# A two-stage recurrent layer on one core: the first stage put in a written order of twelve slots per pair of tiles, its arithmetic taken off GpSimd, and one norm moved to the second stage

## The chip, the cores and the metric

The kernel runs on one core of a Trainium2 chip. A core has five engines that run side by side, each through its own list of instructions in order: TensorE (PE in the profile; PEld is its loading of weights), VectorE (DVE), ScalarE (ACT), GpSimd (POOL) and SyncE (SP), which here only starts transfers. They wait for one another by semaphores. The metric is the device time of one execution in microseconds (us). The kernel before was run three times: 2977.22, 2985.96 and 2986.02 us, so its median is 2985.96 us.

## The reference

One layer over a prompt of 4096 tokens and eight short sequences of 16 tokens, 1024 channels wide:

```
h    = rmsnorm(x, norm_w);  proj = h @ w_in
# group A, gated delta rule, 8 heads of 64
q,k,v = silu(causal_conv(proj[qkv], width 4)); q, k = l2norm(q)/8, l2norm(k)
g    = -exp(A_log) * softplus(a + dt_bias);  beta = sigmoid(b)
#   per chunk: decay = exp(G_i - G_j) for j <= i, G = cumsum(g)
#   lower = strict part of (beta k) k^T * decay; solve (I + lower) [u, w] = rhs
#   v_new = u - w S;  o = (q exp(G)) S + (q k^T * decay) v_new
#   S = S exp(G_last) + (k exp(G_last - G))^T v_new
o_a  = rmsnorm(o, gdn_norm_w) * silu(z_a)        # per head
# group B, HGRN2, 4 heads of 128: forget gate f by channel, same kind of chunked recurrence
o_b  = rmsnorm(o, hgrn_norm_w) * silu(z_b)
y    = rmsnorm(x + concat(o_a, o_b) @ w_out, final_norm_w)
```

The outputs are y for prompt and sequences, the last rows before the convolution, and the final states of both groups.

## The kernel before

The prompt is cut into 32 tiles of 128 tokens; the eight short sequences make one more tile. A group is a pair of prompt tiles, or that one tile: the lone tile comes first, then 16 pairs. Group A runs over all groups in a first stage, group B, the output projection and the last norm in a second one, since both keep the weights of their projections in SBUF.

All projections are done as three fp16 products: weights and x are each split into a high and a low part, and `mm3` (L462–464) adds high·high, high·low and low·high. In the first stage that makes 12 blocks of 128 channels, each 24 matmuls of 128x256 for a pair. What happens to a pair:

- `xload` and `xtrans` (L346–383) load x, norm it (`xss` is the row scale, a power taken by GpSimd at L361, applied at L362) and transpose it into two fp16 parts `xt`. `gate` and `gate2` work out beta and the decays: a polynomial of small operations on VectorE (L405–430), and G along the free axis, sent through DRAM as `gdr`.
- `proj` (L466–515), per block: ScalarE scales the sum `acc` into `u` (L493) and makes two of the four taps of the convolution (L504 from `acc`, L507 from `u`); GpSimd adds these two (L508) and keeps the last three columns in `halo` (L492, L494); VectorE adds the two other taps (L510); ScalarE's tanh (L512) and one VectorE operation (L514) finish silu into `kq` or `vv`.
- `gdn_pre` (L517–582): G is broadcast from DRAM into `E`; GpSimd subtracts (L539) and masks (L540), ScalarE exponentiates; k by token is squared and summed head by head on ScalarE (L554, eight operations with an accumulator per tile); the scores `pk` on TensorE times `E` give `W` and `A` on VectorE (L573, L574); the 32x32 blocks of `W` go to DRAM (`wdr`, L577). `gdn_pre2` makes q and v by token (L594, L600), and GpSimd multiplies `kq` by exp(G) (L602, L603).
- `gdn_inv` (L605–672) inverts the 32x32 triangular blocks of both tiles at once, one system on two partitions. `N` is read back from `wdr` with a transfer that spreads it over the partitions (L623); VectorE scales it (L632) and runs 31 steps of two operations each, L636 (`tm` from `X` and `N`) and L638 (`X` minus `tm`), each needing the one before. `X` then goes through DRAM (`xdr`) into `tx`; VectorE transposes it (L656) and TensorE couples the blocks (`pv`, `px`).
- `gdn_rec` (L674–771) is the recurrence for one tile: `pks` and `po` from the state `S`, then `r` (L713), `py`, `w`, `pcr`, `r` (L723), `pz`, `w`, `pss`, and `S` (GpSimd times its decay at L690, VectorE plus `pss` at L737), each needing the last, back and forth between TensorE, VectorE and ScalarE. The norm of o by head follows: eight squares on ScalarE (L765), a power on GpSimd (L767), a multiplication on VectorE (L769), and `oa` to DRAM (L771).
- `wspill` (L131 on) prepares the weights of the second stage meanwhile, by pieces of 128 columns: GpSimd multiplies by the norm weights (L146) and makes the low part (L185), ScalarE squares and casts; the parts go to DRAM. The first stage's own weights are prepared ahead of its loop by `wprep` (the norm weights at L120, the low part at L129).

The loop over the groups calls these for different groups (transposes for g+2, projection for g+1, preparation for g, recurrence for g−1), but that order is only a suggestion: a scheduler, which simulates the engines with a cost model, decides the order on every engine in both stages. Buffers come from pools that rotate. The second stage (`hg_proj`, `hg_levels`, `hg_tok`, `hg_tile`) is ordered by the same scheduler.

Of the kernel before, what the change touches and what calls it, by code (L numbers as in the profile page):

```python
# [22 lines left out]
XS = 1024.0  # L23


class Kern:
# [10 lines left out]
    # ---------------------------------------------------------------- consts  # L37
    def consts(self, ctx):
# [15 lines left out]
        # small vectors as rows, transposed on the tensor engine  # L54
        i = self.i
        rows = cp.tile([66, P], F32, tag="rows", name="rows")
        nc.sync.dma_start(rows[0:48], i["conv_w"][0].rearrange("t (b p) -> (t b) p", p=P))
        nc.sync.dma_start(rows[48:56], i["norm_w"][0].rearrange("(b p) -> b p", p=P))
        nc.sync.dma_start(rows[56:64], i["hgrn_lb_logits"].rearrange("t (b p) -> (t b) p", p=P))
        nc.sync.dma_start(rows[64:65, 0:64], i["gdn_norm_w"])  # L60
        nc.sync.dma_start(rows[64:65, 64:128], i["gdn_norm_w"])
        nc.sync.dma_start(rows[65:66], i["hgrn_norm_w"])
        self.cols = ct("cols", [P, 66])
        with tc.tile_pool(name="cps", bufs=1, space=PSUM) as pp:
            t = pp.tile([P, 66], F32, tag="t", name="cps_t")
            nc.tensor.transpose(t, rows, self.ident[0:66, 0:66])
            nc.scalar.copy(self.cols, t)
        self.nw = self.cols[:, 48:56]
        self.wosc = self.cols[:, 64:66]
        # conv taps times one half: [p, tap, block]  # L70
# [3 lines left out]
        # -2 exp(A_log), dt_bias on all partitions  # L74
# [6 lines left out]

    def masks(self):
# [3 lines left out]
        # mi[t, i] = t <= i  # L86
# [3 lines left out]
        # sequence of a token of the sample tile: sm[t, s], b16[t, i], ms[t, i] = b16 and t <= i  # L90
# [12 lines left out]
    # --------------------------------------------------------------- weights  # L103
    def wscale(self, tot, us, s2, oscale, small, nm):
        """s2, a power of two: the fp16 parts of weights with that sum of squares; us = oscale / s2"""
# [6 lines left out]
        nc.vector.tensor_scalar(us, us, oscale, None, ALU.mult)  # L112

    def wprep(self, c0, c1, hi, lo, us, stg, eng):
        """hi + lo = (rows of w_in scaled by norm_w) * s in fp16 parts, us = 1 / (s * XS), s a power of two."""
# [4 lines left out]
        eng.tensor_tensor(st, st, self.nw[:, :, None].to_broadcast([P, NDC, w]), ALU.mult)  # L120
# [6 lines left out]
        self.wscale(tot, us, s2, 1.0 / XS, small, c0)  # L127
# [3 lines left out]
    def wspill(self):  # L131
        """the same for the weights of phase B, to DRAM in fp16 parts, by steps of 128 columns"""
# [7 lines left out]
        fac = {}  # L140

        def stage(nm, src, c):
            st = self.ex.tile([P, NDC, P], F32, tag="st", name=f"st{nm}{c}")
            with self.tc.issue_after(self.mark.ins):
                nc.sync.dma_start(st, src[:, :, c:c + P])
            nc.gpsimd.tensor_tensor(st, st, fac[nm][:, :, None].to_broadcast([P, NDC, P]), ALU.mult)  # L146
            return st

        for nm, src, c0 in names:
            fac[nm] = wrow if src is wout else self.nw  # L150
            self.wd[nm] = self.wdp.tile([P, 2, NDC, 512], F16, tag=f"wd{nm}", name=f"wd{nm}")
            ssq = w.tile([P, 4], F32, tag=f"ssq{nm}", name=f"ssq{nm}")
            if nm == "o0":
                # rows of w_out: norm weight of the head and what the gate left out
# [4 lines left out]
            for c in range(4):  # L159
                st = stage(nm, src, c0 + c * P)  # L160
                nc.scalar.activation(st, st, AF.Square, accum_out=ssq[:, c:c + 1])
                yield
# [1030 lines left out]
```

## Time and profile before

| | |
|---|---|
| times of three runs | 2977.22, 2985.96, 2986.02 us |
| the profiled execution's span | 2983.5 us |
| mean granted TensorE clock | 0.943 |
| busy over the span | PE 87%, DVE 59%, ACT 41%, POOL 33% |
| stages, read from where the groups' projections end | to 155.2 us: weights, the lone tile's and the first pair's projection; to 1436.3: the other 15 projections; to 1600: the last pair's rest and the second stage's start; to 2983.5: the second stage |

The profiled execution's own time is not stated apart from its span; the span runs from its first to its last instruction and lies within the range of the runs. Times in the trace count from the span's start. The profile has the busy time and the idle time of each engine, what ended each idle time, and groups of instructions by source line; a duration of a matmul includes its way through a pipeline, so the pitch between neighbours is what it costs. A clock of 1 is TensorE at full speed; 0.5 would be half.

### The profile page before, as it was taken

Reading aid. Unit: us, or ns where it says so; the run is one execution under the profiler, and the core shown is the slowest. Engines: PE = TensorE matmul, PEld = TensorE weight load, DVE = VectorE, ACT = ScalarE, POOL = GpSimd, SP = SyncE. Lnnn points to the kernel's source line nnn. Section 1 sums busy time; section 2 is a strip of 40 time slices with the busy share of each in tenths; the row PEclk is TensorE's granted clock in tenths of the full one; section 3 lists DMA queues with packets and bytes.
Section 4 is the critical chain, followed back from the end, with each engine's and each line's share of the span. In section 5 each row is a group of like instructions: output and inputs, shape, how many; then the busy total and the mean of one; then the engine's idle time right before and its main releaser. Section 6 shows DMA issues by size and latency. Waiting matters only on the chain.

```text
span 2983.5 us, 67579 instructions
## 1 busy us (share of the span) xinstructions
PE 2598.1 (87%) x27628; PEld 1847.4 (62%) x27628; DVE 1752.2 (59%) x4215; ACT 1219.2 (41%) x3930; POOL 991.0 (33%) x1300
## 2 busy tenths in 40 slices
PE   4768678877877887778899999999999999999997
PEld 4656566665666666666674666666656666665664
DVE  7786778777778788876644434444433344433343
ACT  6656565555555665555332222222222222222222
POOL 5755565465565665655320001110001111000110
PEclk9888999888898989888999999999999999999999
DMA  6334232233343333333233231111110111111010
GB/s 180 100 100 122 68 107 74 73 101 106 98 121 77 96 103 99 97 94 115 77 92 112 73 98 40 43 51 44 51 47 24 46 44 50 44 51 34 32 37 33
DMA packets 298701, 227.78 MB, mean 76 GB/s; under 512 B 186409, under 2 KB 263614, under 8 KB 293782
## 3 DMA queue, kind: packets, MB, share of 16 engines
q1 hardware_dynamic: 298390, 223.45, 25.6%
q8 instruction: 217, 3.56, 0.5%
q14 instruction: 94, 0.77, 0.1%
HBM read 151.78 MB, written 71.62 MB: 75 GB/s over the span
## 4 chain that ended last, share of the span: by engine, by line
PE 49%; DVE 28%; DMA 13%; ACT 2%; issue 2%; POOL 2%; SPq 2%; DVEq 0%; POOLq 0%; ACTq 0%
DMA N<-wdr 7%; DVE X L638 6%; DVE c L510 5%; DVE tm L636 5%; PE py L1016 4%; PE py L1014 4%; PE py L1015 4%; PE hac L462 4%; PE hac L464 4%; PE hac L463 4%; PE sc L954 2%; PE tpzb L1014 2%; PE tpza L1014 2%; PE tpzb L1015 2%; PE tpzb L1016 2%
## 5 line engine op out<-in xcount | busy, mean ns | idle before, releaser
L462 PE MATMUL acc<-xt,w 128*128 128x256 f16 (+1 forms) x1632 | 468.9, 289 | 38.5 <-ACT c L504 36.8
L464 PE MATMUL acc<-xt,w 128*128 128x256 f16 (+1 forms) x1632 | 468.0, 288 | 2.7 <-DVE w L129 2.7
L463 PE MATMUL acc<-xt,w 128*128 128x256 f16 (+1 forms) x1632 | 468.9, 289 | 0.0
L510 DVE SCALAR_TENSOR_TENSOR c<-u,cw,c 128x256 f32<-128x256 f32 (+1 forms) x408 | 237.0, 584 | 31.0 <-POOL c L508 29.8
L1145 DVE SCALAR_TENSOR_TENSOR xr<-py,ysc,xr 128x512 f32<-128x512 f32 x66 | 49.5, 750 | 302.3 <-PE py L1016 302.3
L638 DVE TENSOR_TENSOR X<-X,tm 128x126 f32<-128x126 f32 (+26 forms) x527 | 220.5, 418 | 7.3
L512 ACT ACTIVATE c<-c 128x256 f32<-128x256 f32 (+1 forms) x204 | 83.4, 409 | 322.3 <-DVE c L510 197.6
L463 PEld LDWEIGHTS <-w 128*128 128x128 f16 x1632 | 171.9, 105 | 67.8 <-issue 41.3
L1014 PE MATMUL py<-wo,oh 128*128 128x512 f16 x528 | 201.0, 381 | 4.7 <-ACT oh L1137 3.5
L1016 PE MATMUL py<-wo,ol 128*128 128x512 f16 x528 | 201.1, 381 | 0.2
L1015 PE MATMUL py<-wo,oh 128*128 128x512 f16 x528 | 201.0, 381 | 0.0
L462 PEld LDWEIGHTS <-w 128*128 128x128 f16 x1632 | 172.2, 106 | 37.6 <-issue 9.9
L464 PEld LDWEIGHTS <-w 128*128 128x128 f16 x1632 | 172.0, 105 | 33.5 <-issue 3.3
L636 DVE TENSOR_TENSOR tm<-X,N 128x126 f32<-128x126 f32 (+26 forms) x527 | 187.9, 357 | 7.1
L1048 POOL TENSOR_TENSOR zs<-zs,pw_m 128x1 f32<-128x1 f32 x33 | 20.9, 632 | 469.6 <-DVE zs L1047 469.6
L508 POOL TENSOR_TENSOR c<-c,c 128x256 f32<-128x256 f32 (+1 forms) x204 | 155.9, 766 | 50.9 <-ACT c L507 41.8
L462 PE MATMUL hac<-bxt,whq 128*128 128x256 f16 (+1 forms) x544 | 147.4, 273 | 9.0 <-DVE q L924 9.0
L463 PE MATMUL hac<-bxt,whq 128*128 128x256 f16 (+1 forms) x544 | 147.2, 273 | 0.0
L464 PE MATMUL hac<-bxt,whq 128*128 128x256 f16 (+1 forms) x544 | 147.0, 273 | 0.0
L462 PE MATMUL hac<-bxt,whf 128*128 128x256 f16 (+1 forms) x544 | 145.4, 270 | 0.0
L464 PE MATMUL hac<-bxt,whf 128*128 128x256 f16 (+1 forms) x544 | 145.4, 270 | 0.0
L463 PE MATMUL hac<-bxt,whf 128*128 128x256 f16 (+1 forms) x544 | 145.3, 270 | 0.0
(399 smaller groups left out, 6692.3 us busy)
## 6 DMA issues: line engine op xcount, KB each, us to landing
E<-gdr SPq DMA_DIRECT2D x33, 512.0 KB
out_dram<-xr SPq DMA_DIRECT2D x33, 512.0 KB
x<-in_x_prompt_dram SPq DMA_DIRECT2D x32, 512.0 KB
xd<-xt SPq DMA_DIRECT2D x16, 1024.0 KB
bxt<-xd SPq DMA_DIRECT2D x16, 1024.0 KB
xr<-in_x_prompt_dram SPq DMA_DIRECT2D x32, 512.0 KB
tx<-xdr SPq DMA_DIRECT2D x66, 128.0 KB
oa<-on SPq DMA_DIRECT2D x33, 256.0 KB
```

Source lines behind the costliest of these rows:

```text
L462: nc.tensor.matmul(out, wh[k], xh[k], start=(k == 0), stop=False)
L463: nc.tensor.matmul(out, wh[k], xl[k], start=False, stop=False)
L464: nc.tensor.matmul(out, wl[k], xh[k], start=False, stop=(k == n - 1))
L508: nc.gpsimd.tensor_tensor(c, c, c0, ALU.add)
L510: nc.vector.scalar_tensor_tensor(cv, taps[j], self.cw[:, j, b:b + 1], cv, ALU.mult, ALU.add)
L512: nc.scalar.activation(th, c, AF.Tanh)
L636: nc.vector.tensor_tensor(tv, X[:, 0:R, m:m + 1].to_broadcast([2 * SY, R, c]), N[:, m:m + 1, m + 1:32].to_broadcast([2 * SY, R, c]), ALU.mult)
L638: nc.vector.tensor_tensor(X[:, 0:R, m + 1:32], X[:, 0:R, m + 1:32], tv, ALU.subtract)
L954: nc.tensor.matmul(ps[b:b + 32, k, h], KS[:, k, h, b:b + 32], rhs(k, h, slice(b, b + 32)), start=True, stop=True, tile_position=(0, b))
L1014: nc.tensor.matmul(acc, xh[:, dc], wh[dc], start=(dc == 0), stop=False)
L1015: nc.tensor.matmul(acc, xh[:, dc], wl[dc], start=False, stop=False)
L1016: nc.tensor.matmul(acc, xl[:, dc], wh[dc], start=False, stop=(dc == NDC - 1))
```

## The change

The first stage's loop runs under `manual_schedule`: on every engine the instructions keep the order in which the code writes them. The loop over g has 12 slots. In each slot come, in this order: one step of the recurrence of group g−1, the convolution's pending operations, a second step of the recurrence, one block of the projection of g+1 (24 matmuls), one step each of the preparation of g (which goes on into the next round's first slots), of the gates of g+1 and of the transposes of g+2, and in four of the twelve slots a unit of the spill of weights. The rest after the last round, and the second stage, are still left to the scheduler.

What GpSimd computed moves: the third tap becomes a VectorE operation (three L594 per block, one ScalarE tap less), and two blocks share the `u`, tanh and silu operations; E − G becomes a bias of ScalarE's exponential, head by head (16 operations for 2 a pair); the products by exp(G) go to VectorE (L703), the decay of `S` is fused with its addition (L846, eight operations of 64x64 for two of 64x256 and one on GpSimd); the spill's low parts go to VectorE (L197). The norm weights are multiplied into x (L373) and no longer into the weights. GpSimd keeps masks, powers and small copies. The squares by head become one ScalarE square and one VectorE sum over heads (L608). The norm of o leaves the first stage: it stores o and 8 columns of `nrm` (520 columns for 512), and the second stage's `hg_tok` squares, sums, takes the power and multiplies.

```diff
+            with tc.manual_schedule():
+                for g in range(-1, ng):
+                    rec = self.gdn_rec(g - 1, st.pop(g - 1), oa) if g >= 1 else iter(())
...
+                    for s in range(NSLOT):
+                        next(rec, None)
+                        self.conv_jobs()
+                        next(rec, None)
+                        if g + 1 < ng:
+                            self.proj(g + 1, st[g + 1], s)
+                        for it in (*pre, gat, xs):
+                            next(it, None)
+                        if g >= 0 and s in after:
+                            next(spill, None)
...
-                nc.gpsimd.tensor_tensor(lo, st, hi, ALU.subtract)
...
+                nc.scalar.activation(hi, st, AF.Copy, scale=s2[nm])
+                nc.vector.scalar_tensor_tensor(lo, st, s2[nm], hi, ALU.mult, ALU.subtract)
...
-        nc.vector.tensor_scalar(x, x, ss[:, 1:2], None, ALU.mult)
...
+        nc.vector.scalar_tensor_tensor(x, x, ss[:, 1:2], self.nwb, ALU.mult, ALU.mult)
...
+                nc.scalar.activation(E[:, k, h], E[:, k, h], AF.Exp, bias=nG[:, k, h:h + 1])
...
-            nc.gpsimd.tensor_tensor(c, c, c0, ALU.add)
-            for j in (1, 2):
-                nc.vector.scalar_tensor_tensor(cv, taps[j], self.cw[:, j, b:b + 1], cv, ALU.mult, ALU.add)
...
+        for e in range(2):
+            for j in (1, 2, 3):
+                nc.vector.scalar_tensor_tensor(cv[e], taps[e][j], self.cw[:, j, b + e:b + e + 1], cv[e],
+                                               ALU.mult, ALU.add)
...
+    def sums(self, out, x, sq):
+
+        self.nc.scalar.activation(sq, x, AF.Square)
+        yield
+        self.nc.vector.tensor_reduce(out, sq, AX.X, ALU.add)
...
-        nc.gpsimd.tensor_tensor(E, E, d["G"][:, k, :, None].to_broadcast([P, 8, P]), ALU.subtract)
...
-        nc.gpsimd.tensor_tensor(kq[:, k, 4:8], kq[:, k, 4:8], eg, ALU.mult)
-        nc.gpsimd.tensor_tensor(kq[:, k, 0:4], kq[:, k, 0:4], eg, ALU.mult)
...
+            nc.vector.tensor_tensor(qk, qk, d["eg"][k][:, None].to_broadcast([P, 2, 4, P]), ALU.mult)
...
+            if m in (6, 13, 21):
+                yield
...
-                nc.vector.tensor_tensor(S[q, :, q], S[q, :, q], pss[q], ALU.add)
+                for p in range(4):
+                    nc.vector.scalar_tensor_tensor(S[q, p, q], S[q, p, q], el[q, p, DEC_B - 1:], pss[q, p],
+                                                   ALU.mult, ALU.add)
...
-            nc.scalar.activation(junk, po[:, h * 64:(h + 1) * 64], AF.Square, accum_out=n[:, 0, h:h + 1])
...
+        nc.scalar.copy(on[:, 0:512], po)
+        nc.scalar.copy(on[:, 512:520], nrm[:, k, 0:8])
+        nc.sync.dma_start(oa[self.groups[g][k]], on)
...
+            sq = self.ex.tile([P, 8, 64], F32, tag="st", name=f"sq{nm}", bufs=1)
+            o3 = on[:, 0:512].rearrange("p (h d) -> p h d", h=8)
+            nc.scalar.activation(sq, o3, AF.Square)
+            n8 = sm.tile([P, 2, 8], F32, tag="n8", name=f"n8{nm}")
+            nc.vector.tensor_reduce(n8[:, 0], sq, AX.X, ALU.add)
+            nc.vector.scalar_tensor_tensor(n8[:, 0], n8[:, 0], 1.0 / 64, on[:, 512:520], ALU.mult, ALU.add)
+            nc.gpsimd.tensor_tensor(n8[:, 1], n8[:, 0], self.pw_m[:, 0:8], ALU.pow)
+            nc.vector.tensor_tensor(o3, o3, n8[:, 1, :, None].to_broadcast([P, 8, 64]), ALU.mult)
```

How the order changes is seen at three places. Over the whole program VectorE has 4669 instructions for 4217, ScalarE 2044 for 2874, GpSimd 644 for 1302; TensorE and SyncE have as many as before.

VectorE in the middle of the elimination of a pair, before (L636 and L638 are a step's two operations; L376, L514 and L510 belong to other pairs' transposes and convolution):

```order
L376 TENSOR_TENSOR xt_9722<-xtr_0_10265,xt_9722 128x4x128
L636 TENSOR_TENSOR tm_10018<-X_10017,N_10015 128x100
L514 SCALAR_TENSOR_TENSOR kq_10343<-c_0_10528,c_0_10523 128x2x128
L638 TENSOR_TENSOR X_10017<-X_10017,tm_10018 128x4x25
L376 TENSOR_TENSOR xt_9722<-xtr_1_10272,xt_9722 128x4x128
L636 TENSOR_TENSOR tm_10018<-X_10017,N_10015 128x96
```

The same place after the change (L710 and L712 are the two operations):

```order
L710 TENSOR_TENSOR tm_10045<-X_10044,N_10042 128x31
L712 TENSOR_TENSOR X_10044<-X_10044,tm_10045 128x31
L710 TENSOR_TENSOR tm_10045<-X_10044,N_10042 128x30
L712 TENSOR_TENSOR X_10044<-X_10044,tm_10045 128x30
L710 TENSOR_TENSOR tm_10045<-X_10044,N_10042 128x58
L712 TENSOR_TENSOR X_10044<-X_10044,tm_10045 128x2x29
```

Operations of other parts stood between the steps; now the steps of one slot stand one behind the other, in four runs of 14, 14, 16 and 18 operations.

VectorE between the last `W` of a pair, whose store `N` is read back from, and the scaling of `N`; before:

```order
L573 TENSOR_TENSOR WA_1_9988<-pk_1_1_9996,E_9908 128x2x2x128
L574 TENSOR_TENSOR WA_1_9988<-pk_1_1_9996,E_9908 128x2x2x128
L510 SCALAR_TENSOR_TENSOR c_6_10447<-u_6_10446,cw,c_6_10447 128x256
L360 TENSOR_SCALAR xss_10200<-xss_10200 128x1
L510 SCALAR_TENSOR_TENSOR c_6_10447<-u_6_10446,cw,c_6_10447 128x256
L362 TENSOR_SCALAR x_10198<-x_10198,xss_10200 128x1024
L600 TENSOR_TENSOR kv_0_9932<-vt_0_10220,sqk_9906 128x512
L514 SCALAR_TENSOR_TENSOR kq_10343<-c_6_10452,c_6_10447 128x2x128
L596 TENSOR_SCALAR nrm_9905<-nrm_9905 128x8
L600 TENSOR_TENSOR kv_1_9982<-vt_1_10243,sqk_9906 128x512
L632 TENSOR_TENSOR N_10015<-N_10015,cs_10016 128x1024
```

After the change, the last 11 of the 20 rows that stand between the last `W` (L632 there) and the scaling of `N` (L706), and that row:

```order
L700 TENSOR_TENSOR kv_0_9694<-vt_0_10062,sqk_9687 128x512
L703 TENSOR_TENSOR kq_8654<-kq_8654,eg_0_9372 128x1024
L487 TENSOR_TENSOR dec_10141<-nG_10072 128x16
L370 TENSOR_SCALAR xss_10144<-xss_10144 128x1
L602 SCALAR_TENSOR_TENSOR kq_9658<-kq_9658,c_6_10001 128x2x256
L594 SCALAR_TENSOR_TENSOR c_0_10175<-u_0_10174,cw,c_0_10175 128x2x128 x3
L846 SCALAR_TENSOR_TENSOR S<-S,el_0_8462,pss_0_10148 64x64 x8
L608 TENSOR_REDUCE nrm_9686<-sq_1_10134 128x8
L699 TENSOR_SCALAR nrm_9686<-nrm_9686 128x8
L700 TENSOR_TENSOR kv_1_9914<-vt_1_10136,sqk_9687 128x512
L703 TENSOR_TENSOR kq_8654<-kq_8654,eg_1_9378 128x1024
L706 TENSOR_TENSOR N_10042<-N_10042,cs_10043 128x1024
```

The nine rows not shown hold a silu (L602), six taps (L594), an `r` (L819), a norm of x (L373), a low part of the spill (L197), a sum over heads (L608) and two small ones: eight operations stood in this place before, and 33 do now (a row with x3 or x8 is that many).

TensorE at the start of a slot after the change (`pk`, `px` end the slot before; `pks` and `po` begin a tile's recurrence; the rows after them are the projection's next block):

```order
L753 MATMUL px_9802<-tx_0_9452,V_9739 32x32 x16
L753 MATMUL px_9802<-tx_1_9455,V_9739 32x32 x16
L779 MATMUL pks_9861<-S,kq_7650 128x128 x4
L781 MATMUL po_9860<-S,kq_7650 128x128 x4
L525 LDWEIGHTS w_181
L525 MATMUL acc_6_9884<-xt_8746,w_181 128x256
L526 LDWEIGHTS w_181
L526 MATMUL acc_6_9884<-xt_8746,w_181 128x256
```

The block's 24 matmuls stand between `pks`, whose result VectorE turns into `r`, and `py`, which needs `r`. So it is with each of the recurrence's four trips between TensorE and another engine.

More of the change, by code (lines that the diff above doesn't have):

```diff
@@ L1 @@
+from collections import deque
 from contextlib import ExitStack
@@ L325, in phase_a @@
+            akq.close()
+            self.b_begin(xd)
+            for it in (*pre, self.gdn_rec(ng - 1, st.pop(ng - 1), oa)):
+                for _ in it:
+                    pass
             for par in range(2):
```

648 lines of the change are left out of this document (352 added, 296 removed).

## The prediction

> **What bounds the kernel now.** I first read the table by stretches: the stretch's length, then busy time (and count) of PE, PEld, DVE, ACT and POOL, the granted clock, the share and rate of the DMA engines.
>
> ```profile
> 0.00:155.20 155.20, 94.62 (x841) 78.69 (x842) 120.39 (x308) 95.45 (x252) 98.62 (x126) 0.90 0.49 138
> 155.20:1436.30 1281.10, 996.71 (x11283) 815.84 (x11283) 1002.05 (x2449) 742.63 (x2684) 726.95 (x959) 0.89 0.36 99
> 1436.30:1600.00 163.70, 142.43 (x1803) 102.35 (x1799) 80.01 (x224) 49.34 (x194) 35.69 (x44) 0.95 0.33 96
> 1600.00:2983.50 1383.50, 1364.32 (x13711) 850.50 (x13709) 549.80 (x1237) 331.81 (x802) 129.74 (x172) 1.00 0.14 47
> ```
>
> The second stage is TensorE's: 1364 of 1383.5 us. The first is nobody's, with PE and DVE level at 78% and two engines behind. Its second row covers 15 pairs, 85.4 us each (1281.1/15): PE 66.4, DVE 66.8 busy and 18.6 idle, ACT 49.5, POOL 48.5. The same stretch, for the projection's sums alone, PE then ACT:
>
> ```profile
> 155.20:1436.30 1281.10, 570.37 (x4288) 155.66 (x360) 0.89 0.36 99
> ```
>
> That is 38.0 us of PE per pair, so 28.4 us for the rest. What DVE waited for there (us in all, times, longest):
>
> ```profile
> DVE N L632 <- DMA N<-wdr: 143.7, 14, 13.3
> DVE tT L656 <- DMA tx<-xdr: 41.1, 22, 4.2
> DVE c L510 <- POOL c L508: 25.5, 19, 3.4
> ```
>
> Per pair 9.6, 2.7 and 1.7 us: 14.0 of the 18.6. The chain of waits over one pair shows the first (start, length):
>
> ```profile
> 1280.26 0.61 DVE WA L573
> ...
> 1285.11 13.06 DMA N<-wdr
> ```
>
> From the start of the last W to the landing of N pass 17.9 us (1285.11 + 13.06 − 1280.26), and DVE runs dry before that. So DVE's time, busy plus these waits, sets the pair.
>
> **GpSimd inside DVE's busy time.** The same stretch by groups (busy, mean ns | idle), and then minimum, median and maximum of single instructions over the run:
>
> ```profile
> L510 DVE SCALAR_TENSOR_TENSOR c<-u,cw,c 128x256 f32<-128x256 f32 x362 | 213.3, 592 | 26.6 <-POOL c L508 25.5
> L638 DVE TENSOR_TENSOR X<-X,tm 128x126 f32<-128x126 f32 (+23 forms) x469 | 200.1, 427 | 6.1
> L636 DVE TENSOR_TENSOR tm<-X,N 128x126 f32<-128x126 f32 (+23 forms) x468 | 167.7, 358 | 5.9
> L514 DVE SCALAR_TENSOR_TENSOR kq<-c,c 128x256 f32<-128x256 f32 x120 | 68.6, 572 | 7.4 <-ACT c L512 7.2
> ```
>
> ```profile
> L510 DVE SCALAR_TENSOR_TENSOR c<-u,cw,c x408: 336/478/2354, 48.9 to 1432.6; 128x256 f32<-128x256 f32 x128, 128x128 f32<-128x128 f32 x8
> L638 DVE TENSOR_TENSOR X<-X,tm x527: 158/273/2255, 108.5 to 1486.3; 128x126 f32<-128x126 f32 x16, 128x78 f32<-128x78 f32 x11, 128x120 f32<-128x120 f32 x11, 128x96 f32<-128x96 f32 x11
> L636 DVE TENSOR_TENSOR tm<-X,N x527: 158/265/2196, 108.0 to 1486.1; 128x126 f32<-128x126 f32 x16, 128x78 f32<-128x78 f32 x11, 128x120 f32<-128x120 f32 x11, 128x96 f32<-128x96 f32 x11
> L514 DVE SCALAR_TENSOR_TENSOR kq<-c,c x136: 292/418/2309, 54.0 to 1416.6; 128x256 f32<-128x256 f32 x128, 128x128 f32<-128x128 f32 x8
> ```
>
> The means lie far above the medians: 362×0.114 + 469×0.154 + 468×0.093 + 120×0.154 = 41 + 72 + 44 + 18 = 175 us, 11.7 per pair. The timeline says why: a DVE row of 1.98 us, then the GpSimd row beside it.
>
> ```profile
> 798.98 0.48 DVE L510 SCALAR_TENSOR_TENSOR c<-u,cw,c 128x256 f32<-128x256 f32 x1
> 799.38 0.24 DVE L636 TENSOR_TENSOR tm<-X,N 128x78 f32<-128x78 f32 x1
> ...
> 803.39 1.98 DVE L638 TENSOR_TENSOR X<-X,tm 128x115 f32<-128x115 f32 x1
> ...
> 842.16 0.99 DVE L510 SCALAR_TENSOR_TENSOR c<-u,cw,c 128x256 f32<-128x256 f32 x2
> ```
>
> ```profile
> 803.35 1.90 POOL L539 TENSOR_TENSOR E<-E,Gc 128x1024 f32<-128x1024 f32 x1 [0.42 <-ACT eg L538]
> ```
>
> GpSimd starts 0.04 us ahead, and DVE's L638, some 0.27 us of work, ends 0.12 us after it. With the groups not shown I put the stall at 16 us per pair, an estimate (11.7 is its lower bound).
>
> By the Trainium skill (SBUF — State Buffer, the list under its diagram) a VectorE instruction with two SBUF inputs and a GpSimd instruction that reads SBUF lock each other out for a whole instruction; the row above agrees (1.98 us), and by that the masks would go on stalling.
>
> **The change, DVE per pair.** Three more rows give prices, the fourth what GpSimd still does beside small ones:
>
> ```profile
> L573 DVE TENSOR_TENSOR WA<-pk,E 128x512 f32<-128x512 f32 x59 | 40.3, 682 | 0.5 <-PE pk L571 0.2
> L737 DVE TENSOR_TENSOR S<-S,pss 64x256 f32<-64x256 f32 x56 | 23.3, 416 | 1.4 <-PE pss L733 0.5
> L632 DVE TENSOR_TENSOR N<-N,cs 128x1024 f32<-128x1024 f32 x15 | 19.0, 1269 | 153.4 <-DMA N<-wdr 143.7 <-DMA cs<-cdr 9.8
> ```
>
> ```profile
> L540 POOL TENSOR_SCALAR_AFFINE_SELECT E<-E 128x1024 f32<-128x1024 f32 x30 | 34.7, 1156 | 0.0
> ```
>
> - Taps: the tap at 798.98 lets the next operation, which doesn't need it, start after 0.40 us, 0.08 before its own end; the two at 842.16, the second needing the first, take 0.99, a pitch of 0.51. Before 24×0.40 = 9.6; now three in a chain for each of 12 blocks, 12×(0.51+0.51+0.40) = 17.0: **+7.4**.
> - Elimination: the same 62 operations, now each behind the one it needs, so up to 0.11 us more each, 6.8. Some stood so before (the order shows it at 128x96): **+4** (0 to 6.8).
> - Four sums over heads at L573's 0.68: **+2.7**. Two products by exp(G) at L632's 1.27: **+2.5**.
> - S: sixteen of 64x64, no row of that size; the smallest operations take 0.16 (the minimum of L636), 16×0.17 = 2.7 for 4×0.42 = 1.7: **+1.0** (up to +5 at L737's 0.42 each).
> - Spill: 28 low parts and 16 products with the weights of the output, 44×1.27/15: **+3.7**. The norm weights make x's product a two-tensor operation: **+0.5** (up to 2.5, L632's whole price twice). Norm of o: **−1.7** (two of L573's size, two small).
> - Stalls: of the arithmetic 16 us go; the masks stay, 2×1.16 us of GpSimd for E, of which I let 1.5 stall: **−14.5** (−10 to −16).
>
> Sum +5.6, so 66.8 becomes 72.4 busy. On ScalarE a tap goes, squares lose their accumulators, sixteen exponentials come: it stays under its 49.5 and doesn't bound. PE's work is the same 66.4.
>
> **DVE's waits.** Of the 18.6, taps no longer wait for GpSimd (−1.7). `tx` is used three slots after its load is issued, 20 us at 82/12 a slot, against a wait of at most 4.2: −2.7. Between the last W and N stand 33 operations for 8: nine taps 4.3, two silu of 512 1.4, `r` 0.7, x, the spill's part and two exp(G) products 5.1, two sums and two L700 2.7, S 1.4, small ones 0.8: 16.4 against 17.3 us from the end of W. But SyncE's list is fixed too: N's load stands there behind the stores of W, two stores and a load of the spill and the store of the factors `cs`, whose transpose PE makes behind the slot's block of the projection, 38.0/12 = 3.2 us; if PE isn't ahead, N is that much later (and cs with it), and the elimination, and everything DVE has queued behind L706, waits. I leave 1.5 of the 9.6 (0 to 4). The other 4.6 of the 18.6 stay. New are waits that a fixed order makes: DVE may stand before an operation whose producer is late though others are ready. The nearest row is L514's idle above, 7.2 us in 15 pairs; a chain through one `pk` buffer and two through GpSimd's powers come to about 3.5 a pair at some 0.5 to 1 each. Bounds: 0, and what the rivals say. So P = 72.4 + 1.5 + 4.6 + 3.5 = 82.0 us, −3.4 × 15 = **−51**.
>
> **Outside the loop.** Scaling the first weights goes (DVE, then GpSimd, to 155.2 us):
>
> ```profile
> L120 DVE TENSOR_TENSOR wst<-wst,cols 128x2048 f32<-128x2048 f32 (+1 forms) x4 | 7.1, 1787 | 2.1 <-DMA wst<-in_w_in_dram 2.1
> ```
>
> ```profile
> L120 POOL TENSOR_TENSOR wst<-wst,cols 128x2048 f32<-128x2048 f32 x3 | 12.5, 4160 | 2.9 <-DMA wst<-in_w_in_dram 2.9
> ```
>
> At most 20 us, at least none: I take −10. The 163.7 us between the stages keep their scheduler and their work: 0. In the second stage 33 tiles get two DVE operations of 0.68, an ACT square and a GpSimd power, under a TensorE busy 98.6%, with DVE 60% idle: +3 (0 to 20). Total −51 − 10 + 3 = −58 from the profiled 2983.5: 2925.5 us. That execution's span is 2.5 under the median of the runs, so I say **2928**.
>
> **Rivals.**
>
> *Nearly no waits.* If the order is good enough that the new waits and most of the 4.6 go, P is about 75.5: −149 − 7, 2828. For it: 24 matmuls stand between every two steps of the recurrence. Against: each engine's list is strict now.
>
> *The chained order is free.* Then the +4 and 24×0.11 = 2.6 of the taps vanish: P 75.4, −150 − 7, 2827. The 0.99 for two taps against 0.40 for one speaks against it. The Trainium skill says so (VectorE: DVE Perf Modes, The DRAIN you can't avoid: the next operation waits until the pipeline is empty, and a semaphore between costs nothing more); the rows differ, since at 799.38 the next operation started 0.08 us before the recorded end.
>
> *The trips of the recurrence stall both lists.* What PE waited for before:
>
> ```profile
> PE py L718 <- DVE r L713: 38.5, 10, 12.4
> PE pz L726 <- DVE r L723: 20.4, 9, 5.7
> PE pks L685 <- DVE S L737: 19.9, 8, 6.4
> ```
>
> On average 2.9 us (78.8/27). A scheduler put these waits anywhere; now eight trips per pair each stand before a block, and behind a late `r` wait py, the block after it, the sums of the convolution and then DVE. PE has little slack to catch up when it then runs slower (0.89 granted already). If four of the eight trips cost DVE 2.9 us, the new waits are 11.6 for 3.5, P 90.1: +70 − 7, 3047. It decides from new waits of about 7.5 us. For it: the 62 chained operations, 62×0.30 = 19 us, lie in four slots, so with a third of the other 53 DVE has 37 us there against 27 of a pair's 82, while PE's blocks are even. Against: the block between.
>
> *The stalls are not GpSimd's arithmetic.* Without the 14.5, P is 96.5: +166 − 7, 3143. The pair of rows at 803 speaks against.
>
> *The second stage waits for o.* ScalarE's square of `on` must wait for its load, and behind it stand the casts that TensorE needs; at 2.9 us a tile, 33×2.9 = 96: 3022. Against: ACT there is busy 24%, and a scheduler still orders it.
>
> *It cancels:* new waits of 6.5 to 8 us, within 0.3% of 2986.
>
> **Chances.** Forecast 0.50, with its own range 2873 to 2971 (new waits 0 to 6.5); nearly no waits 0.14; free chains 0.05; cancels 0.09; trips 0.14; second stage 0.05; stalls elsewhere 0.03. A measurement tells about 0.3% from no change: faster 0.50 + 0.14 + 0.05 = 0.69, same 0.09, slower 0.22. The range, 2815 to 3040, holds both cheap cases and the second stage's, and leaves out half of the trips, the stalls elsewhere and the tails of the cheap cases, under 2 in 10.
>
> **What would show it.** The step from one pair's projection to the next near 82 us; DVE busy near 72 in it; median and mean of the taps and the elimination together, with long ones only beside the masks; the wait of L706 for N under 4 us; no wait for GpSimd's sum. PE waiting for `r` in most pairs, or a lower clock than 0.89, would be the trips; a TensorE share well under 98.6% after 1600 us the second stage. The prediction is wrong if DVE's idle time a pair is over 13 us, or its busy time over 76.

## The result: 2.3% slower

| | median us | runs |
|---|---|---|
| before | 2984.73 | 2977.22 to 2986.02 |
| after the change | 3050.49 | 3048.78 to 3060.57 |

The median of before now counts the profiled execution, 2983.5, as a fourth time. The ratio is 1.023, with a 95% interval of 1.021 to 1.025. The prediction was 2928 us, with a range up to 3040: wrong in sign, and just outside its range.

The stretch of the profile after that holds the 15 pairs, and the second stage; the columns are as in the prediction's first view. The cuts of the 15 pairs, here and in the table ahead of the change, were counted from another zero than the traces' rows and stand 11 us late: from the span's start the first and the last pair's projections end at 150.7 and 1495.7 us (144.0 and 1425.0 before, not 155.2 and 1436.3). The stretches have the right length, and VectorE's busy time in them is the same within 1 us.

```profile
161.80:1507.00 1345.20, 1018.35 (x11370) 856.10 (x11368) 1084.50 (x2788) 566.77 (x1226) 195.34 (x349) 0.87 0.34 95
```

```profile
1665.00:3049.10 1384.10, 1364.12 (x13704) 849.86 (x13702) 586.73 (x1326) 345.63 (x830) 182.56 (x202) 1.00 0.14 47
```

A pair takes 1345.2/15 = 89.7 us (85.4 before): VectorE is busy for 72.3 and idle for 17.4, TensorE busy for 67.9. The second stage stays at its 1384 us with TensorE busy 98.6%, so the norm that moved there costs nothing that shows. Of the 65.6 us by which the profiled span grew (3049.1 − 2983.5), 64 lie in these 15 pairs, 6.7 ahead of them and −5 behind.

What VectorE waits for in that stretch (us in all, times, longest):

```profile
DVE c L594 <- ACT c L591: 61.4, 53, 3.2
DVE xss L370 <- ACT xt L367: 58.6, 14, 7.7
DVE WA L632 <- PE pk L627: 31.9, 30, 2.7
...
DVE tT L737 <- DMA tx<-xdr: 3.6, 7, 1.0
DVE N L706 <- DMA cs<-cdr: 3.5, 1, 3.5
```

The three waits of before are gone: `N` had 143.7 us and now has one wait of 3.5, `tx` had 41.1 and has 3.6, GpSimd's tap isn't there. In their place stand three that were small before: the taps behind ScalarE's first tap (no such wait before), x's norm behind ScalarE's square of x (5.0 us before), and `W` behind the scores (0.2). Together they are 151.9 us, 10.1 a pair.

### The profile page after: what moved, and what is told of

It is laid out like the page before. It is cut to its first block, busy times and chain, and to the rows that moved or that the text cites. A ratio compares the mean times of both kernels' runs of the same rounds, so it can differ in the third digit from the quotient of the medians.

```text
span 3049.1 us, 65219 instructions
## 1 busy us (share of the span) xinstructions
PE 2618.9 (86%) x27628; PEld 1885.2 (62%) x27628; DVE 1867.5 (61%) x4667; ACT 1029.2 (34%) x2308; POOL 431.1 (14%) x642
## 4 chain that ended last, share of the span: by engine, by line
PE 55%; DVE 25%; ACT 7%; DMA 6%; issue 4%; POOL 2%; SPq 1%; POOLq 0%; ACTq 0%; DVEq 0%
DVE c L594 6%; DVE tm L710 4%; DVE X L712 4%; PE py L1117 4%; PE py L1115 4%; PE py L1116 4%; PE hac L527 4%; PE hac L525 3%; PE hac L526 3%; PE sc L1055 2%; PE tphi L1115 2%; PE tpzb L1115 2%; PE tpza L1115 2%; PE tphi L1116 2%; PE tphi L1117 2%
## 5 line engine op out<-in xcount | busy, mean ns | idle before, releaser
L525 PE MATMUL acc<-xt,w 128*128 128x256 f16 (+1 forms) x1632 | 479.6, 296 | 11.2 <-ACT u L577 6.4
L526 PE MATMUL acc<-xt,w 128*128 128x256 f16 (+1 forms) x1632 | 476.7, 294 | 0.0
L527 PE MATMUL acc<-xt,w 128*128 128x256 f16 (+1 forms) x1632 | 474.2, 293 | 0.3 <-DVE w L145 0.3
L594 DVE SCALAR_TENSOR_TENSOR c<-u,cw,c 128x256 f32<-128x256 f32 (+1 forms) x612 | 313.3, 513 | 92.7 <-ACT c L591 78.2
L525 PEld LDWEIGHTS <-w 128*128 128x128 f16 x1632 | 175.4, 108 | 40.9 <-ACT w L144 1.5
L526 PEld LDWEIGHTS <-w 128*128 128x128 f16 x1632 | 174.9, 107 | 39.0 <-issue 10.2
L527 PEld LDWEIGHTS <-w 128*128 128x128 f16 x1632 | 175.1, 107 | 32.1 <-DVE w L145 0.5
L600 ACT ACTIVATE kq<-c 128x512 f32<-128x512 f32 (+1 forms) x68 | 41.9, 617 | 387.3 <-DVE c L594 387.2
L710 DVE TENSOR_TENSOR tm<-X,N 128x126 f32<-128x126 f32 (+26 forms) x527 | 139.8, 265 | 16.7
L712 DVE TENSOR_TENSOR X<-X,tm 128x126 f32<-128x126 f32 (+26 forms) x527 | 138.5, 263 | 17.9
L1259 ACT ACTIVATE oh<-xr 128x1024 f16<-128x1024 f32 x33 | 34.9, 1057 | 311.8 <-DVE xr L1257 311.8
L1116 PEld LDWEIGHTS <-bxt 128*128 128x128 f16 x792 | 78.3, 99 | 95.9 <-issue 15.3
```

The lines of the kernel that those rows point to most:

```text
L525: nc.tensor.matmul(out, wh[k], xh[k], start=(k == 0), stop=False)
L526: nc.tensor.matmul(out, wh[k], xl[k], start=False, stop=False)
L527: nc.tensor.matmul(out, wl[k], xh[k], start=False, stop=(k == n - 1))
L594: nc.vector.scalar_tensor_tensor(cv[e], taps[e][j], self.cw[:, j, b + e:b + e + 1], cv[e], ALU.mult, ALU.add)
L600: nc.scalar.activation(dst, ck, AF.Tanh)
L710: nc.vector.tensor_tensor(tv, X[:, 0:R, m:m + 1].to_broadcast([2 * SY, R, c]), N[:, m:m + 1, m + 1:32].to_broadcast([2 * SY, R, c]), ALU.mult)
```

## What the pairs show before any experiment

From the matmuls of the projection, the 15 pairs after the change take 96, 84, 82, 84, 92, 92, 89, 92, 92, 89, 92, 95, 96, 85 and 83 us. The three of 82 to 84 and the last two are quicker than a pair of before on the mean (85.4). The nine of 89 to 96 in the middle are those in whose rounds the spill either multiplies by the output's weights or writes its parts. VectorE's low parts are 1.28 us each and its products 1.22, four a pair of the one or the other, and of both in the pairs of 95 and 96. So 5 us, in those two 10, are VectorE's own work; the rest must be waiting. One such pair, first ScalarE, then VectorE, then GpSimd (start, length, idle time before and what ended it):

```profile
908.37 0.60 ACT L606 ACTIVATE sq<-qt 128x512 f32<-128x512 f32 x1 [7.33 <-DMA wdhf<-hihf]
908.86 0.21 ACT L488 ACTIVATE dec<-dec 128x16 f32<-128x16 f32 x1
908.97 1.05 ACT L367 ACTIVATE xt<-x 128x1024 f16<-128x1024 f32 x1
...
911.48 0.91 ACT L591 ACTIVATE c<-u,cw 128x256 f32<-128x256 f32 x2 [0.80 <-POOL u L576]
```

```profile
910.13 0.15 DVE L370 TENSOR_SCALAR xss<-xss 128x1 f32<-128x1 f32 x1 [7.63 <-ACT xt L367]
910.21 0.68 DVE L602 SCALAR_TENSOR_TENSOR kq<-kq,c 128x512 f32<-128x512 f32 x1
912.02 1.52 DVE L594 SCALAR_TENSOR_TENSOR c<-u,cw,c 128x256 f32<-128x256 f32 x3 [1.14 <-ACT c L591]
```

```profile
910.44 0.87 POOL L371 TENSOR_TENSOR xss<-xss,pw_m 128x1 f32<-128x1 f32 x1 [16.06 <-DVE xss L370]
911.26 0.19 POOL L576 COPY u<-halo 128x6 f32<-128x6 f32 x1
```

ScalarE stands 7.33 us before the square of q, because the buffer for its result is one of three `on` buffers that it shares with the spill's parts, and a store of such a part to DRAM still reads it. Behind the square stands the square of x; VectorE stands 7.63 us for it; GpSimd's power stands for VectorE; behind the power stands the small copy into `u`; ScalarE's first tap stands for the copy, and VectorE's taps for that. One late store stops three lists.

## The experiments

Times are compared with the kernel before on the same chip. "Busy", "overlap" and the gaps are VectorE's, per pair over the 15 pairs, worked out from the start and length of each of its instructions: the union of the instructions, how much of their lengths lies on top of the one before, gaps under 0.06 us, and longer ones. Busy time and the two kinds of gaps add up to the pair.

| kernel | us | ratio to before | pair | busy | overlap | gaps under 0.06 | longer gaps |
|---|---|---|---|---|---|---|---|
| before | 2983 to 2987 | 1 | 85.4 | 66.9 | 9.4 | 1.1 | 17.4 |
| after | 3050 | 1.023 [1.021, 1.025] | 89.7 | 72.3 | 4.9 | 4.0 | 13.4 |
| square of q in `vs` | 3006 | 1.008 [1.006, 1.010] | 86.9 | 72.3 | 4.9 | 4.0 | 10.7 |
| halo copies on ScalarE | 3039 | 1.019 [1.018, 1.021] | 89.0 | 72.1 | 4.9 | 3.9 | 12.9 |
| taps a slot later | 3125 | 1.049 [1.047, 1.052] | 95.1 | 72.2 | 5.0 | 3.9 | 19.0 |
| scheduler's order | 2933 | 0.983 [0.982, 0.985] | 81.7 | 64.0 | 11.0 | 1.2 | 16.5 |
| taps alternating | 3027 | 1.014 [1.012, 1.016] | 87.9 | 70.5 | 6.8 | 3.1 | 14.3 |
| elimination alternating | 2998 | 1.004 [1.003, 1.006] | 87.0 | 70.7 | 6.4 | 3.3 | 13.0 |
| the last two and `vs` | 2957 | 0.991 [0.989, 0.992] | 83.2 | 69.3 | 7.9 | 2.7 | 11.2 |
| + spill split | 2948 | 0.987 [0.985, 0.989] | 83.7 | 69.5 | 8.1 | 2.7 | 11.6 |
| + halo on ScalarE | 2933 | 0.982 [0.980, 0.984] | 82.8 | 68.8 | 8.2 | 2.7 | 11.4 |
| + first pair by scheduler | 2942 | 0.985 [0.982, 0.987] | 85.6 | 70.0 | 8.3 | 2.7 | 13.0 |
| scheduler's order, `vs` | 2971 | 0.996 [0.994, 0.997] | 83.0 | 63.4 | 10.0 | 1.5 | 18.2 |
| exp product on GpSimd | 3062 | 1.026 [1.023, 1.028] | 90.7 | 73.0 | 4.8 | 4.0 | 13.8 |

Two theories stood against each other first: that the written order's waits come from single late operations at the head of a list (a buffer, a small copy), and that they come from the recurrence's trips between the engines, as the prediction's rival had it.

### The square of q out of the shared buffer

```diff
-            sums = self.sums(nrm[:, k, 0:8], qt, self.onb(f"sq{g}_{k}")[:, 0:512].rearrange("p (h d) -> p h d", h=8))
+            sums = self.sums(nrm[:, k, 0:8], qt, d["T"][k][3])
```

> Edit: the square of q goes into the tile's vs buffer (free then), not into one of the three rotating on buffers, which it shares with the spill's parts. Theory of the shared buffer: the profile of the change shows ScalarE waiting 47 us in all for stores of the spill's parts before that square (7.3 us a time), and behind it the square of x, for which VectorE's L370 waits 58.6 us. Then the wait of L370 falls to about 10 us and the time by 35 to 50 us, to about 3005. Theory of the trips (TensorE waiting for r and S, 214 us in the stretch, sets the pair): these waits only move, and the time stays within 10 us of 3050.

Measured: 3006 us, 44 less. VectorE's waits with it:

```profile
DVE c L594 <- ACT c L591: 63.4, 53, 3.4
DVE WA L632 <- PE pk L627: 31.1, 29, 2.3
DVE xss L370 <- ACT xt L367: 18.5, 14, 1.3
```

The wait of x's norm falls from 58.6 to 18.5 us, the time by about as much, and the pairs in which the input weights' parts are written fall from 89 to 92 to 83 to 86 us. So the buffer's cause is shown. The recurrence's waits, TensorE's in the kernel after, were these:

```profile
PE pz L823 <- DVE r L819: 80.9, 14, 7.5
PE pks L779 <- DVE S L846: 72.8, 14, 9.1
PE py L811 <- DVE r L805: 60.7, 16, 8.5
```

By the prediction's own sign (TensorE waiting for `r` in most pairs, or a clock under 0.89; it was 0.87) these trips would be the cause. Three things speak against it. VectorE's own list has no wait for `pks`, `pcr` or a pair's `pss`. In the chain of waits that ended last, a wait of TensorE for `r` stands once in these 15 pairs, with 11.6 us of TensorE behind it, and none for a pair's `S`. And the three waits don't go with the time: they add up to 214 us after the change, 188 with this edit, 149 in the kernel with three edits below and 168 in the best written order, which is 24 us quicker than that one. The 149 are these:

```profile
PE pz L854 <- DVE r L36: 92.6, 14, 9.1
PE pks L810 <- DVE S L36: 28.1, 14, 2.5
PE py L842 <- DVE r L36: 27.8, 16, 5.5
```

The clock doesn't decide either: in the scheduler's order below it was 0.85 over the 15 pairs, and they were quicker. So waiting for `r` and `S` is not what costs. But the chain isn't VectorE's alone any more: it lies on TensorE for 20% of these pairs, 2% before. The largest piece, 106 us, are eight stretches that begin with `pks` behind the end of the inversion (ScalarE's `tx`) and go on along TensorE's list.

### GpSimd's small copies

```diff
-            nc.gpsimd.tensor_copy(u[:, :, 0:3], self.halo[:, bb])
+            nc.scalar.copy(u[:, :, 0:3], self.halo[:, bb])
...
-            nc.gpsimd.tensor_copy(self.halo[:, bb], u[:, :, N:])
+            nc.scalar.copy(self.halo[:, bb], u[:, :, N:])
```

> Edit: the two small copies of the convolution's last columns go from GpSimd to ScalarE. Theory of GpSimd's single list: the copy into u stands behind the power of x's norm, which waits for VectorE, so ScalarE's first tap waits 51.9 us for it and VectorE's taps 59.3 us for that. Then the taps' wait falls to about 20 us and the time by 25 to 45 us, to about 3015. If VectorE's wait is only ScalarE being late by itself, the wait stays near 55 and the time within 10 us of 3050; if the twelve extra ScalarE copies of a pair (some 2.5 us) count, it is longer.

Measured: 3039, 11 less. Over 200 to 1430 us the taps' wait falls from 55.1 to 35.2 us, not to 20, and less of it arrives in the time than was expected: x's norm waits for 64.2 us instead of 57.3, and ScalarE, with the copies, is busy for 1.1 us more a pair.

### The taps one slot later

```diff
             nc.scalar.activation(cv[e], taps[e][0], AF.Copy, scale=self.cw[:, 0, b + e:b + e + 1])
+        yield
```

> Edit: VectorE's taps of a block come one slot after ScalarE's first tap instead of in the same slot. If VectorE's wait at the taps (59.3 us) is what costs, whatever made ScalarE late, it falls under 10 us and the time by 40 to 60 us, to about 3000. If the wait only stands in for another one that VectorE would reach next (scores, the recurrence, x's norm), the time falls by less than 20 us.

The lone tile's last two blocks of v come a slot too late with this edit, so its preparation reads them (`vt` on TensorE, 90.5 us) before the operation that finishes their silu (91.7 us); the instructions are otherwise the same. Measured: 3125, 75 more, which neither expectation had. VectorE's waits over 200 to 1430 us, and one of ScalarE:

```profile
DVE xt L386 <- ACT xt L385: 76.4, 13, 6.0
DVE xss L370 <- ACT xt L367: 66.4, 12, 7.6
DVE WA L633 <- PE pk L628: 35.1, 26, 2.4
...
ACT xt L385 <- PE xtr L383: 81.8, 25, 6.6
```

The taps hardly wait any more (1.1 us), but the list now waits at x's transposes, which ScalarE copies late, and ScalarE there waits for TensorE (6.2 us in the kernel after). Where that starts is open. One reading from the code, not tried: ScalarE's tanh of one pair of blocks, which waits for VectorE's taps, now stands directly ahead of the next pair's `u`, so that ScalarE is a turn later everywhere. The wait's own place says little about what to change.

### The same instructions in the scheduler's order

```diff
-            with tc.manual_schedule():
+            with ExitStack():
```

> Edit: the written order is taken away, the scheduler orders the same instructions. Theory that the strict order costs and the moved arithmetic gains (VectorE free of GpSimd's stalls): about 2930 to 2970, under the kernel before. Theory that the moved arithmetic is what costs (VectorE's work grew to 72 us a pair): 3030 or more.

Measured: 2933, under the kernel before, as the first theory of this expectation had it. With the same 4667 VectorE instructions the busy time of the whole run (the page's first part, of the kernel after, then of this one) differs by 128.6 us:

```profile
PE 2618.9 (86%) x27628; PEld 1885.2 (62%) x27628; DVE 1867.5 (61%) x4667; ACT 1029.2 (34%) x2308; POOL 431.1 (14%) x642
```

```profile
PE 2599.1 (89%) x27628; PEld 1872.0 (64%) x27628; DVE 1738.9 (59%) x4667; ACT 1026.6 (35%) x2308; POOL 461.2 (16%) x642
```

In the first stage alone (3203 instructions) the lengths of VectorE's instructions add up to 1320 us after and 1291 here; the overlap of neighbours is 83 against 182, the gaps under 0.06 us 67 against 23, and the longer gaps 327 against 381. So the written order did take 54 us of real waiting away. It lost 99 of overlap, 44 of short gaps and 28 of length: 171 − 54 = 117, the difference of the two times. What the scheduler's order still waits for is what the written one had mended:

```profile
DVE N L706 <- DMA cs<-cdr: 111.6, 11, 15.2
DVE N L706 <- DMA N<-wdr: 38.1, 3, 12.9
```

### The chained operations taken apart

The written order's elimination, one operation behind the one that it needs:

```profile
928.03 0.29 DVE L712 TENSOR_TENSOR X<-X,tm 128x126 f32<-128x126 f32 x1
928.36 0.28 DVE L710 TENSOR_TENSOR tm<-X,N 128x120 f32<-128x120 f32 x1
928.68 0.28 DVE L712 TENSOR_TENSOR X<-X,tm 128x120 f32<-128x120 f32 x1
```

Each starts 0.03 to 0.04 us after the last one's end: 0.32 us an operation of 0.28. The first edit lets the six taps of two blocks alternate, in the same slots:

```diff
-        for e in range(2):
-            for j in (1, 2, 3):
-                nc.vector.scalar_tensor_tensor(...)
-            if e == 0:
-                yield
+        for n_, (j, e) in enumerate(((1, 0), (1, 1), (2, 0), (2, 1), (3, 0), (3, 1))):
+            if n_ == 3:
+                yield
+            nc.vector.scalar_tensor_tensor(...)
```

> Edit: the six taps of two blocks, which stand as two chains of three, alternate between the two blocks, three in each of the same two slots. Theory of the chained order (VectorE's next operation starts 0.08 us before the recorded end of one that it doesn't need, 0.03 us after the end of one that it needs; in the first stage the written order has 83 us of such overlap against 182 us in the scheduler's order of the same instructions): 24 operations a pair gain 0.11 us, 2.6 us a pair, so VectorE's busy time falls by about 40 us and the time by 25 to 40, to about 3015. If only waits for other engines set the pair, the busy time falls and idle time takes its place: within 8 us of 3050.

The second puts the elimination's operations into a list `todo`, of which one is issued behind each other VectorE operation of the slots, and the rest at a slot's end (slots 6 to 9, batches of 16, 20 and 26 operations):

```diff
-            nc.vector.tensor_tensor(X[:, 0:R, m + 1:32], X[:, 0:R, m + 1:32], tv, ALU.subtract)
-            if m in (6, 13, 21):
-                yield
+            self.todo.append(lambda m=m, R=R, tv=tv: vec.tensor_tensor(
+                X[:, 0:R, m + 1:32], X[:, 0:R, m + 1:32], tv, ALU.subtract))
+            if m in (7, 17, 30):
+                yield
+                while self.todo:
+                    self.todo.popleft()()
...
+            r = f(*a, **kw)
+            if self.todo:
+                self.todo.popleft()()
```

> Edit: the elimination's operations are put one by one behind VectorE's other operations of slots 6 to 9, as far as there are any, the rest in a row at the slot's end. About half of the 62 then stand apart. Theory of the chained order: 30 x 0.11 = 3.3 us a pair, VectorE's busy time down by some 50 us, the time by 30 to 50, to about 3010. If waits set the pair: within 8 us of 3050; if the recurrence's r, now with eliminations between, comes later, longer.

Measured: 3027, 24 less, and 2998, 53 less. Each takes a little under 2 us of busy time a pair away (72.3 to 70.5 and 70.7), 1.8 × 16 = 29 and 1.6 × 16 = 26 us, and 0.9 and 0.7 of short gaps. In the second kernel, where VectorE's other operations of this stage all bear line 36, the alternating part reads:

```profile
910.30 0.28 DVE L741 TENSOR_TENSOR X<-X,tm 128x130 f32<-128x130 f32 x1
910.51 0.48 DVE L36 SCALAR_TENSOR_TENSOR c<-u,cw,c 128x256 f32<-128x256 f32 x1
910.90 0.28 DVE L738 TENSOR_TENSOR tm<-X,N 128x120 f32<-128x120 f32 x1
```

The elimination's operation of 0.28 us costs 0.21 here, a tap of 0.48 costs 0.39. So the chained order costs, and its price per operation is the prediction's 0.11. Of the 2.7 us by which a pair fell with the second edit, busy time and short gaps make 2.3; the waits at the taps and at x's norm stayed (60.0 and 59.6 us, 61.4 and 58.6 without the edit). But the 15 pairs give only 39 of the 49 us between the two profiled executions; the others lie ahead of the pairs and behind them, and why stays open.

> Edit: the square of q in vs, the taps and the elimination alternating, together. Theory that buffer and chained order each cost by themselves: 3050 - 44 - 35 - 40 = about 2930, under the kernel before. If what VectorE saves turns into waits for ScalarE and for the scores: 2965 to 3000.

Measured: 2957, 93 less than after and 0.9% under the kernel before. That is between the two expectations. The three gains alone add up to 121, or to 114 in the profiled executions, which differ by 99 here. Of the 15 us that are missing there, 10 lie in the 15 pairs, in busy time and short gaps; the longer gaps are 11.2 us a pair, as the three edits add up to. So the savings didn't turn into waits.

### Two more waits, and the best written order

```diff
                 nc.vector.tensor_tensor(st, st, wrow[:, :, None].to_broadcast([P, NDC, P]), ALU.mult)
+            yield
...
-                        if g >= 0 and s in after:
+                        if g >= 0 and (s in after or s - 1 in after):
```

> Edit: f3, and VectorE's product of a unit of the spill with the output's weights comes one slot ahead of ScalarE's square or cast of it, instead of in the same slot. In f3 ScalarE waits 23.1 and 22.5 us for these products (16 units), and the four pairs with them take 86 to 91 us against 80 to 82 of the others. Theory that ScalarE's list stands behind these waits: those four pairs fall to about 83, the time by 20 to 28 us, to about 2933. If these pairs are longer for VectorE's added work alone (1.2 us a unit, 5 us a pair): less than 8 us.

Measured: 2948, 10 less, under what was expected of it. ScalarE's waits for these products fall from 45.6 to 1.8 us, and the four pairs from 86 to 91 to 83 to 85; but others rose, to 85 and one from 81 to 90, and the pair took 83.7 on the mean for 83.2. The gain is ahead of these pairs: the first one's projection ended at 132.6 us instead of 147.6. Why is open.

> Edit: f4, and the copies of the convolution's last columns on ScalarE. Its gain alone was 11 us (3039 for 3050). If it adds: 11 us under f4. With the pairs at 80 us the taps' wait (61 us in f3) is a larger share: up to 25 us.

Measured: 2933, 14 less. This kernel (the written order with the square in `vs`, the taps and the elimination alternating, the spill's product a slot ahead, the copies on ScalarE) is 1.8% under the kernel before, level with the scheduler's order of the same arithmetic. It still waits for the scores and the same two as before, and the chain of waits that ended last now lies on TensorE for 38% of the 15 pairs (20% after the change), so VectorE alone no longer tells what the next edit is worth:

```profile
DVE WA L36 <- PE pk L654: 37.2, 30, 2.4
DVE xss L36 <- ACT xt L395: 35.1, 14, 2.8
DVE c L36 <- ACT c L619: 19.6, 20, 4.2
```

> Edit: f5, and the first two rounds of the loop (the lone tile's projection and the first pair's) without the written order. The first pair's projection ended at 162 us after the change, at 155 before, and at 116 under the scheduler with the same arithmetic. Theory that twelve slots hold the first pair back, since the lone tile's chain of waits fills them: it ends at 115 to 130 us and the time falls by 20 to 35 us against f5. If the work is only shifted (the scheduler's kernel had 47 us more behind its last projection): within 8 us of f5.

Here the loop's first two rounds stand outside `manual_schedule`. Measured: 2942, 9 more than without. From the span's start the first pair's projection ended at 101 us instead of 133 (the ends in the expectation are 11 us late as well), and the next one took 112 us instead of 90: the work is only shifted, and the theory that the slots hold the first pair back falls.

### Is it the arithmetic after all?

```diff
-            nc.vector.tensor_tensor(qk, qk, d["eg"][k][:, None].to_broadcast([P, 2, 4, P]), ALU.mult)
+            nc.gpsimd.tensor_tensor(qk, qk, d["eg"][k][:, None].to_broadcast([P, 2, 4, P]), ALU.mult)
```

> Edit: the kernel after the change, with one piece of its arithmetic back on GpSimd: k and q times exp(G), 128x1024, two a pair. VectorE has 2 x 1.23 = 2.5 us a pair less to do. Theory that GpSimd's two-input work stalls VectorE: two operations of about 2.6 us each stall it up to 5.2 us a pair, so its busy time rises by 0 to 2.7 us and the time is the same or up to 40 us longer than 3050. If there is no such stall: 25 to 40 us shorter.

Measured: 3062, 12 more. That is not clear of noise (the intervals of the two ratios overlap); that it isn't 25 to 40 shorter is. GpSimd takes 2.37 us each, VectorE loses two operations of 1.22 a pair and is busy for longer (73.0 for 72.3): it stands for GpSimd for some 3 us a pair, half of it in the taps, whose mean goes from 513 to 556 ns. The taps' row is first that of the kernel after, then this one's.

```profile
L703 POOL TENSOR_TENSOR kq<-kq,eg 128x1024 f32<-128x1024 f32 x33 | 78.2, 2369 | 5.1 <-PE qt L638 3.9
```

```profile
L594 DVE SCALAR_TENSOR_TENSOR c<-u,cw,c 128x256 f32<-128x256 f32 (+1 forms) x612 | 313.3, 513 | 92.7 <-ACT c L591 78.2
```

```profile
L594 DVE SCALAR_TENSOR_TENSOR c<-u,cw,c 128x256 f32<-128x256 f32 (+1 forms) x612 | 340.1, 556 | 95.8 <-ACT c L591 81.2
```

So this move off GpSimd is not what costs; the loss is the order's, as the scheduler's order of the same instructions showed. How much the move is worth under a scheduler is less sure:

> Edit: the scheduler's order and the square of q in vs. Theory that the shared buffer costs because a written order can't go round the waiting square: no gain under the scheduler, 2933 within 8 us. If the buffer costs in any order: 2890 to 2915.

Measured: 2971, 38 more than the scheduler's order without the edit, though the edit only frees a buffer. Neither expectation holds. The scheduler laid out the pairs differently (54 to 113 us each, 57 to 117 without the edit), so two orders of the same work that it finds lie 38 us apart, and the moved arithmetic is worth between 15 and 50 us there (2971 and 2933 against 2986 and 2983, the medians of before beside them).

## Why the prediction was wrong, by its own steps

- **VectorE's busy time, 72.4 us: 72.3 measured.** The stalls went as forecast: by the excess of each instruction over the quick ones of its form they were 18.0 us a pair before and 2.3 after, for 16 and 1.5. The chained operations' price was right in kind and size, 0.32 us for one of 0.28, where 0.21 is possible. But the sum counted the gaps of 0.03 between chained operations as busy, and the profile counts them as idle. Busy time and short gaps together grew from 68.0 to 76.3 us a pair, 8.3 for the forecast 5.6: the 36 taps cost 18.9 us (0.53 from start to start) for 17.0, and S cost more (0.65 us for three, 16 a pair: 3.5 for 2.7).
- **`N`, `tx` and GpSimd's tap: right.** `N` was left 1.5 us a pair and has 0.2; `tx` was left none and has 0.2.
- **"New waits 3.5 us": the step that failed.** The row it was sized by, L514's wait for ScalarE, comes from the scheduler's order and not from a written one. Measured were 10.1 us in three waits (4.1 taps, 3.9 x's norm, 2.1 scores). A pair took 89.7 us instead of 82.0, which makes 116 of the 124 us by which the profiled span missed its sum: of the 7.7 us, 5.0 are waiting (the longer gaps fell by 4.0 us instead of 9.0) and 2.7 the sum of the point above. VectorE's idle time of 17.4 us is beyond the 13 that the prediction named as its sign of being wrong. The largest single part of the waits, 44 us of time, is a thing that the prediction didn't look at: which buffers a rotating pool hands to operations of different engines, and that a store holds them.
- **The start: −10 forecast, +6.7 measured.** The scaling of the weights did go (the lone tile's projection ended at 66.5 us instead of 80.3), but the first pair's then took twelve slots, 84 us instead of 64. The one other order that was tried at the start didn't gain it back.
- **The second stage: +3 forecast, nothing measured**, and what stands behind the last projection was 5 us shorter in all.
- **The rivals.** The trips' time, 3047 (3049 with the 2.5 us that the forecast adds), is nearly the measured one, but by another mechanism: VectorE didn't wait for the recurrence. Its sign came (TensorE waited for `r` in most pairs) and misled; a list did stand behind one late operation, but not behind that one. Nearly no waits, a second stage that waits and a sum that cancels did not come about. That chained order is free is refuted: taking part of the chains apart gave 24 and 53 us. The stalls were GpSimd's arithmetic.

By the Trainium skill (VectorE: DVE Perf Modes, The DRAIN you can't avoid) the next operation can't start before the pipeline is empty, and a semaphore between two costs nothing more; the section also says that a next operation that isn't held starts earlier. The rows here agree with the last: an independent operation starts 0.07 to 0.09 us before the recorded end of the one ahead. A dependent one starts 0.03 to 0.04 after it, so a dependence does cost here, the 0.11 us.

## What to carry to other kernels

A written order is as good as its lists' heads: before fixing one, follow for each engine what stands behind every operation that can be late, including operations that wait only for a buffer, and give results that wait for a store a buffer of their own. On VectorE, set chains of short dependent operations apart with independent ones; in this kernel an operation of 0.28 us costs 0.32 in a chain and 0.21 between others, and the two edits that did this gained 24 and 53 us, together more than the 54 us of waiting that the written order took away. When a change fixes the order and moves work at once, run the moved work under the old order too: here that alone gave a gain, of 15 to 50 us.

## What was not expected of the hardware

GpSimd's masks, which read SBUF, cost VectorE little once the arithmetic had gone (2.3 us a pair of all stalls, with 4.5 us of masks, 43.5 + 24.5 over 15 pairs). And VectorE's busy time is not a measure of its work: the same 3203 instructions filled 1236 us in one order and 1109 in another, though they differ by only 28 us in the sum of their lengths.
